# Interleaved rotary embedding, one core: six batch rows on chip instead of five, VectorE in pieces of four positions

## Chip, cores, metric

One core of a Trainium2 chip. The metric is the device time of one execution in microseconds, the median of several; lower is better.

## The reference

`x` is (8, 2048, 16, 64) in float32: 8 batch rows, 2048 positions, 16 heads, 64 values a head. `cos` and `sin` are (2048, 32). Each neighbouring pair of a head is rotated by its position's angle:

```python
x1, x2 = x_pairs[..., 0], x_pairs[..., 1]
out1 = x1 * cos - x2 * sin
out2 = x1 * sin + x2 * cos
out = np.stack([out1, out2], axis=-1).reshape(batch, seq_len, num_heads, head_dim)
```

Input and output are 67.1 MB each, one batch row 8.39 MB each way.

## The kernel before

Partition p holds positions 16p to 16p + 15 (K = 16) of a batch row, 16,384 values. A row comes in through a DMA that GpSimd issues (line 57) and that turns float32 into bf16 on the way; it is rotated in place by VectorE and goes out through a DMA that GpSimd issues (line 60), which turns bf16 into float32. `buf` holds NX = 5 rows of 32 KB a partition, and `at` says in which place a batch row lies; rows 5, 6 and 7 reuse the places of rows 0, 1 and 2.

`rotate` does a stretch of positions in three VectorE operations: the product with the sine table into `qt` (line 79), the product with the cosine table in place (line 85), and the sum of the latter and the pairwise swapped `qt` in place (line 91). Both tables are built in bf16 from cos and sin at the start (lines 104 to 106), with the sign of the sine in the table.

Two pieces of row 0 and row 7 go separately. The first four positions of row 0 come in as float32 through a DMA of ScalarE's queue, beside GpSimd's, and VectorE casts them (line 102). The last four positions of row 7 are summed straight into float32 (`tail`) and go out through SyncE's queue (line 136). A copy of one element before them (line 134) makes them wait for the store of row 6.

The order is written out by hand (`manual_schedule`): each engine runs its own instructions in the order of the text, and a DMA waits on its issuing engine for what it depends on. So GpSimd's order is also the order of its DMA queue: loads of 0 (less the four positions), cos, sin, 1, 2; store 0; loads 3 and 4 as one, 5; stores 1 and 2 as one, 3; loads 6 and 7 as one; stores 4 and 5 as one, 6, 7 (less the last four positions).

When the first store is issued is set by a gate: in the first product of row 1, after 14 of 16 positions (GATE), VectorE copies one element of row 0 onto itself (line 84), and the store of row 0 depends on that copy.

Of the kernel before, what the change touches and what calls it, by code (L numbers as in the profile page):

```python
# [2 lines left out]

# [4 lines left out]


@with_exitstack  # L10
def kernel(
    ctx: ExitStack,
    tc: tile.TileContext,
    x: bass.AP,
    cos: bass.AP,
    sin: bass.AP,
    out: bass.AP,
):
    nc = tc.nc
    fp32 = mybir.dt.float32  # L20
    bf16 = mybir.dt.bfloat16
    mult = mybir.AluOpType.mult
    add = mybir.AluOpType.add

    B, S, H, D = x.shape
    P = 128
    K = S // P
    D2 = D // 2
    HD = H * D
    NX = 5  # L30
    HEAD = 4
    TAIL = 4
    GATE = 14

    x_t = x.rearrange("b (p k) h d -> p b k (h d)", p=P, k=K)
    out_t = out.rearrange("b (p k) h d -> p b k (h d)", p=P, k=K)
    cos_t = cos.rearrange("(p k) c -> p (k c)", p=P, k=K)
    sin_t = sin.rearrange("(p k) c -> p (k c)", p=P, k=K)

    consts = ctx.enter_context(tc.tile_pool(name="consts", bufs=1))  # L40
    rows_pool = ctx.enter_context(tc.tile_pool(name="rows", bufs=1))
    stage = ctx.enter_context(tc.tile_pool(name="stage", bufs=1))

    cos_sb = consts.tile([P, K * D2], fp32)
    sin_sb = consts.tile([P, K * D2], fp32)
    c_tab = consts.tile([P, K, D], bf16)
    s_tab = consts.tile([P, K, D], bf16)


    buf = rows_pool.tile([P, NX, K, HD], bf16, name="xt")  # L50
    at = [4, 0, 1, 2, 3, 4, 0, 1]

    def place(b, n=1, k0=0, k1=K):
        return buf[:, at[b] : at[b] + n, k0:k1]

    def load(b, n=1, k0=0, k1=K):
        nc.gpsimd.dma_start(out=place(b, n, k0, k1), in_=x_t[:, b : b + n, k0:k1])  # L57

    def store(b, n=1, k0=0, k1=K):
        nc.gpsimd.dma_start(out=out_t[:, b : b + n, k0:k1], in_=place(b, n, k0, k1))  # L60

    def rotate(b, k0=0, k1=K, gate=None, to=None):
        nk = k1 - k0
        xp = buf[:, at[b], k0:k1]
        qt = stage.tile([P, K, HD], bf16, name="qt", tag="work")

        def rows(a):
            return a.rearrange("p k (h e) -> p k h e", h=H, e=D)

        def tab(a, j0=0, j1=nk):  # L70
            return dataclasses.replace(
                a,
                offset=a.offset + (k0 + j0) * D,
                ap=[a.ap[0], [D, j1 - j0], [0, H], [1, D]],
            )


        for a, z in ((0, nk),) if gate is None else ((0, GATE), (GATE, nk)):
            nc.vector.tensor_tensor(  # L79
                out=rows(qt[:, a:z]), in0=rows(xp[:, a:z]), in1=tab(s_tab, a, z), op=mult  # L80
            )
            if z < nk:
                one = buf[:1, at[gate], 0, :1]
                nc.vector.tensor_copy(out=one, in_=one)  # L84
        nc.vector.tensor_tensor(out=rows(xp), in0=rows(xp), in1=tab(c_tab), op=mult)  # L85
        q_swap = dataclasses.replace(
            qt, offset=qt.offset + 1, ap=[qt.ap[0], [2, nk * HD // 2], [-1, 2]]
        )
        x3 = xp.rearrange("p k (a j) -> p (k a) j", j=2)
        y3 = x3 if to is None else to.rearrange("p k (a j) -> p (k a) j", j=2)  # L90
        nc.vector.tensor_tensor(out=y3, in0=x3, in1=q_swap, op=add)  # L91

    with tc.manual_schedule():
        head = stage.tile([P, TAIL, HD], fp32, name="st", tag="work")
        nc.scalar.dma_start(out=head[:, :HEAD], in_=x_t[:, 0, :HEAD])
        load(0, k0=HEAD)
        nc.gpsimd.dma_start(out=cos_sb, in_=cos_t)  # L97
        nc.gpsimd.dma_start(out=sin_sb, in_=sin_t)  # L98
        load(1)
        load(2)  # L100

        nc.vector.tensor_copy(out=buf[:, at[0], :HEAD], in_=head[:, :HEAD])  # L102
        s2 = s_tab.rearrange("p k (i j) -> p (k i) j", j=2)
        nc.vector.tensor_copy(out=s2[:, :, 0], in_=sin_sb)  # L104
        nc.vector.tensor_scalar_mul(s2[:, :, 1], sin_sb, -1.0)  # L105
        nc.vector.tensor_copy(  # L106
            out=c_tab.rearrange("p k (i j) -> p (k i) j", j=2),
            in_=cos_sb.to_broadcast([P, K * D2, 2]),
        )

        rotate(0, 0, HEAD)
        rotate(0, HEAD, K)
        rotate(1, gate=0)
        store(0)
        load(3, 2)
        load(5)
        rotate(2)
        store(1, 2)
        rotate(3)
        store(3)  # L120
        load(6, 2)
        rotate(4)
        rotate(5)
        store(4, 2)
        rotate(6)
        store(6)
        rotate(7, 0, K - TAIL)
        store(7, k1=K - TAIL)

        tail = buf[:, at[3], : 2 * TAIL].rearrange("p k e -> p (k e)").bitcast(fp32)
        tail = tail.rearrange("p (k e) -> p k e", e=HD)
        nc.vector.tensor_copy(out=buf[:1, at[6], 0, :1], in_=buf[:1, at[7], K - 1, :1])  # L134
        rotate(7, K - TAIL, K, to=tail)
        nc.sync.dma_start(out=out_t[:, 7, K - TAIL :], in_=tail)


# [1 line left out]
_INS = ['x', 'cos', 'sin']  # L140
_OUTS = [((8, 2048, 16, 64), 'float32')]


# [23 lines left out]
```

## Time and profile before

| | |
|---|---|
| median of 3 runs | 316.18 us (316.11 to 316.2) |
| profiled execution, its own time | 316.17 us |
| its span, first to last instruction | 314.4 us |
| VectorE (DVE) busy | 215.4 us, 37 instructions |
| GpSimd (POOL) busy | 8.6 us, 18 instructions |
| DMA, GpSimd's queue (q0) | 2400 packets, 96.8% of the 16 engines' span |
| DMA, ScalarE's and SyncE's queues (q10, q1) | 144 packets each, 1.8% and 1.6% |
| HBM | 67.63 MB read, 67.11 MB written |

The profile's page has 40 equal slices of the span with the busy share of each engine in tenths. The timeline names each instruction with its start, its duration and, in brackets, the idle time of its engine before it and what ended that. A line number is that of the kernel it belongs to; the change moves lines, so the same operation has another number afterwards.

### The profile page before, as it was taken

The page shows a single profiled execution, that of the slowest core. Times are in us where ns is not written, and L with a number is a line of the kernel's source. Part 1 is how long each engine was busy: PE and PEld are TensorE (multiplying, and loading weights), DVE is VectorE, ACT ScalarE, POOL GpSimd, SP SyncE. Part 2 cuts the span into 40 slices and gives each one's busy share as a digit, 9 for nine tenths or more (in the row PEclk, how much of TensorE's full clock was granted, in tenths as well). Part 3 has the DMA queues.
Part 4 walks back from the last instruction along what each step waited for, and adds up shares of the span by engine and source line. Part 5 has one row for each costly group of instructions (what it writes and reads, how often), then busy time and mean ns, then how long its engine had stood idle before and what let it go on. Part 6 is the DMA issues. An engine that isn't in the chain of part 4 may idle for free.

```text
span 314.4 us, 113 instructions
## 1 busy us (share of the span) xinstructions
DVE 215.4 (69%) x37; POOL 8.6 (3%) x18
## 2 busy tenths in 40 slices
DVE  0029999999999206999999999300009999980550
POOL 3000000100000000000000000000000000000000
DMA  8999999999999999999999999999999999999996
GB/s 253 264 284 200 200 204 263 267 400 417 317 200 200 208 258 200 200 284 517 400 400 475 459 400 400 242 225 200 200 300 434 400 400 534 400 400 400 434 500 267
DMA packets 2688, 102.24 MB, mean 325 GB/s; under 512 B 256, under 2 KB 256, under 8 KB 384
## 3 DMA queue, kind: packets, MB, share of 16 engines
q0 software_dynamic: 2400, 98.04, 96.8%
q10 hardware_dynamic: 144, 2.10, 1.8%
q1 hardware_dynamic: 144, 2.10, 1.6%
HBM read 67.63 MB, written 67.11 MB: 429 GB/s over the span
## 4 chain that ended last, share of the span: by engine, by line
DVE 62%; another core or an unknown queue 17%; DMA 17%; issue 0%; POOL 0%; DVEq 0%; PEldq 0%
DVE xt L91 21%; DVE xt L85 20%; DVE qt L79 20%; DMA out_dram<-xt 10%; DMA sin_sb<-in_sin_dram 7%; POOL xt L57 0%; DVE c_tab L106 0%; POOL cos_sb L97 0%; DVE s_tab L104 0%; DVE s_tab L105 0%; DVE xt L134 0%; DVE xt L84 0%; DVEq L79 0%; PEldq L162 0%
## 5 line engine op out<-in xcount | busy, mean ns | idle before, releaser
L79 DVE TENSOR_TENSOR qt<-xt,s_tab 128x16384 bf16<-128x16384 bf16 (+4 forms) x11 | 69.9, 6360 | 53.7 <-DMA xt<-in_x_dram 53.5
L91 DVE TENSOR_TENSOR xt<-xt,qt 128x16384 bf16<-128x16384 bf16 (+3 forms) x10 | 72.0, 7198 | 0.3
L85 DVE TENSOR_TENSOR xt<-xt,c_tab 128x16384 bf16<-128x16384 bf16 (+2 forms) x10 | 69.9, 6986 | 0.3
L102 DVE CAST xt<-st 128x4096 bf16<-128x4096 f32 x1 | 2.3, 2295 | 15.2 <-DMA st<-in_x_dram 15.2
L60 POOL DMA_DIRECT2D out_dram<-xt x6 | 3.6, 604 | 221.0 <-DVE xt L91 165.3
L134 DVE COPY xt<-xt 1x1 bf16<-1x1 bf16 x1 | 0.1, 144 | 12.0 <-DMA out_dram<-xt 12.0
L57 POOL DMA_DIRECT2D xt<-in_x_dram x6 | 3.8, 635 | 53.1 <-DMA out_dram<-xt 52.3
L104 DVE CAST s_tab<-sin_sb 128x512 bf16<-128x512 f32 x1 | 0.5, 451 | 6.3 <-DMA sin_sb<-in_sin_dram 6.3
L106 DVE CAST c_tab<-cos_sb 128x1024 bf16<-128x1024 f32 x1 | 0.7, 682 | 0.0
L98 POOL DMA_DIRECT2D sin_sb<-in_sin_dram x1 | 0.6, 562 | 0.0
L97 POOL DMA_DIRECT2D cos_sb<-in_cos_dram x1 | 0.6, 554 | 0.0
L105 DVE TENSOR_SCALAR s_tab<-sin_sb 128x512 bf16<-128x512 f32 x1 | 0.4, 441 | 0.0
L84 DVE COPY xt<-xt 1x1 bf16<-1x1 bf16 x1 | 0.1, 136 | 0.0
L151 POOL MEMSET const-float32-0.0<- 128x1 f32 x1 | 0.1, 98 | 0.2 <-issue 0.2
L151 POOL MEMSET const-bfloat16-1.0<- 128x1 bf16 x1 | 0.1, 101 | 0.0
L151 POOL MEMSET const-float32-1.0<- 128x1 f32 x1 | 0.1, 98 | 0.0
L151 POOL MEMSET const-uint8-127<- 128x1 uint8 x1 | 0.1, 98 | 0.0
## 6 DMA issues: line engine op xcount, KB each, us to landing
xt<-in_x_dram POOLq DMA_DIRECT2D x2, 8192.0 KB, 58.7
xt<-in_x_dram POOLq DMA_DIRECT2D x3, 4096.0 KB, 57.4
out_dram<-xt POOLq DMA_DIRECT2D x1, 6144.0 KB, 26.2
xt<-in_x_dram POOLq DMA_DIRECT2D x1, 3072.0 KB, 21.2
st<-in_x_dram ACTq DMA_DIRECT2D x1, 2048.0 KB, 14.5
out_dram<-xt SPq DMA_DIRECT2D x1, 2048.0 KB, 10.2
cos_sb<-in_cos_dram POOLq DMA_DIRECT2D x1, 256.0 KB, 21.3
sin_sb<-in_sin_dram POOLq DMA_DIRECT2D x1, 256.0 KB, 21.4
```

The source lines that it names most:

```text
L57: nc.gpsimd.dma_start(out=place(b, n, k0, k1), in_=x_t[:, b : b + n, k0:k1])
L60: nc.gpsimd.dma_start(out=out_t[:, b : b + n, k0:k1], in_=place(b, n, k0, k1))
L79: nc.vector.tensor_tensor(out=rows(qt[:, a:z]), in0=rows(xp[:, a:z]), in1=tab(s_tab, a, z), op=mult)
L85: nc.vector.tensor_tensor(out=rows(xp), in0=rows(xp), in1=tab(c_tab), op=mult)
L91: nc.vector.tensor_tensor(out=y3, in0=x3, in1=q_swap, op=add)
L97: nc.gpsimd.dma_start(out=cos_sb, in_=cos_t)
L98: nc.gpsimd.dma_start(out=sin_sb, in_=sin_t)
L102: nc.vector.tensor_copy(out=buf[:, at[0], :HEAD], in_=head[:, :HEAD])
L104: nc.vector.tensor_copy(out=s2[:, :, 0], in_=sin_sb)
L105: nc.vector.tensor_scalar_mul(s2[:, :, 1], sin_sb, -1.0)
L106: nc.vector.tensor_copy(out=c_tab.rearrange("p k (i j) -> p (k i) j", j=2), in_=cos_sb.to_broadcast([P, K * D2, 2]),)
L151: nc = _bacc.Bacc("TRN2", target_bir_lowering=False, num_devices=1)
```

## The change

`buf` has six places. Rows 0 to 5 have a place each, and rows 6 and 7 reuse those of rows 0 and 1. GpSimd's order becomes: loads of 0, cos, sin, 1, 2 and 3 as one, 4 and 5 as one; stores 0 and 1 as one, 2 and 3 as one; loads 6 and 7 as one; stores 4 and 5 as one, 6, 7. To find the room, `qt` holds four positions (KP) instead of sixteen, so that every row is rotated in four pieces, three VectorE operations each; and the float32 head, cos and sin lie in row 5's place until the tables are made, so that the load of rows 4 and 5 stands behind the tables. The gate moves to the second piece of row 3, after one position, and holds back the store of rows 0 and 1.

```diff
-    NX = 5
+    NX = 6
+    KP = 4
-    GATE = 14
+    GATE = 1
...
-    cos_sb = consts.tile([P, K * D2], fp32)
-    sin_sb = consts.tile([P, K * D2], fp32)
...
-    at = [4, 0, 1, 2, 3, 4, 0, 1]
+    at = [0, 1, 2, 3, 4, 5, 0, 1]
...
-        qt = stage.tile([P, K, HD], bf16, name="qt", tag="work")
+        qt = stage.tile([P, KP, HD], bf16, name="qt", tag="work")
...
-        head = stage.tile([P, TAIL, HD], fp32, name="st", tag="work")
-        nc.scalar.dma_start(out=head[:, :HEAD], in_=x_t[:, 0, :HEAD])
+
+        def fp32_in(b, k0, k1):
+            return buf[:, at[b], k0:k1].rearrange("p k e -> p (k e)").bitcast(fp32)
+
+        head = fp32_in(5, 0, 2 * HEAD).rearrange("p (k e) -> p k e", e=HD)
+        cos_sb = fp32_in(5, K - 2, K - 1)
+        sin_sb = fp32_in(5, K - 1, K)
+        nc.scalar.dma_start(out=head, in_=x_t[:, 0, :HEAD])
...
         load(1)
-        load(2)
+        load(2, 2)
...
-        rotate(0, 0, HEAD)
-        rotate(0, HEAD, K)
-        rotate(1, gate=0)
-        store(0)
-        load(3, 2)
-        load(5)
-        rotate(2)
-        store(1, 2)
-        rotate(3)
-        store(3)
+        load(4, 2)
+
+        def rotate_row(b, k1=K, gate=None):
+            for k in range(0, k1, KP):
+                rotate(b, k, k + KP, gate if k == KP else None)
+
+        rotate_row(0)
+        rotate_row(1)
+        rotate_row(2)
+        rotate_row(3, gate=0)
+        store(0, 2)
+        store(2, 2)
         load(6, 2)
-        rotate(4)
-        rotate(5)
+        rotate_row(4)
+        rotate_row(5)
         store(4, 2)
-        rotate(6)
+        rotate_row(6)
         store(6)
-        rotate(7, 0, K - TAIL)
+        rotate_row(7, K - TAIL)
         store(7, k1=K - TAIL)
...
-        tail = buf[:, at[3], : 2 * TAIL].rearrange("p k e -> p (k e)").bitcast(fp32)
-        tail = tail.rearrange("p (k e) -> p k e", e=HD)
+        tail = fp32_in(3, 0, 2 * TAIL).rearrange("p (k e) -> p k e", e=HD)
```

More of the change, by code (lines that the diff above doesn't have):

```diff
@@ L99 @@
         load(1)
-        load(2)
-        nc.vector.tensor_copy(out=buf[:, at[0], :HEAD], in_=head[:, :HEAD])
+        load(2, 2)
+        nc.vector.tensor_copy(out=buf[:, at[0], :HEAD], in_=head)
         s2 = s_tab.rearrange("p k (i j) -> p (k i) j", j=2)
```

## The prediction, made before the changed kernel ran

> **What bounds the kernel now.** I read the page's slices and queues first. In the slices, each digit is the busy share of the 16 DMA engines in a fortieth of the span.
>
> ```profile
> DMA  8999999999999999999999999999999999999996
> ...
> q0 software_dynamic: 2400, 98.04, 96.8%
> ...
> HBM read 67.63 MB, written 67.11 MB: 429 GB/s over the span
> ```
>
> The DMA engines are busy from the first slice to the last, nearly all on one queue, the one GpSimd fills. VectorE is busy 69%, so it can only matter where it makes a queue run empty. The second view is a table of stretches: start and end, length, VectorE busy, GpSimd busy, clock, DMA share, GB/s.
>
> ```profile
> 81.20:139.10 57.90, 41.68 (x6) 1.27 (x2) 1.00 1.00 216
> 139.10:197.10 58.00, 57.80 (x7) 1.27 (x2) 1.00 1.03 437
> ```
>
> The first stretch is loads alone (rows 3, 4, 5), the second stores alone (rows 1, 2, 3). Three rows take 58 us either way. The load's GB/s is half because it is counted in the 2-byte values that land; a row is 8.39 MB in memory in both directions. Third, the timeline (start, duration, instruction, in brackets the idle time before it), to see whether the queue ever ran dry.
>
> ```profile
> 25.13 2.28 DVE L79 TENSOR_TENSOR qt<-xt,s_tab 128x4096 bf16<-128x4096 bf16 x1
> 27.45 2.29 DVE L85 TENSOR_TENSOR xt<-xt,c_tab 128x4096 bf16<-128x4096 bf16 x1
> 29.77 2.29 DVE L91 TENSOR_TENSOR xt<-xt,qt 128x4096 bf16<-128x4096 bf16 x1
> 32.10 6.56 DVE L79 TENSOR_TENSOR qt<-xt,s_tab 128x12288 bf16<-128x12288 bf16 x1
> ...
> 51.88 7.63 DVE L79 TENSOR_TENSOR qt<-xt,s_tab 128x14336 bf16<-128x14336 bf16 x1
> 59.42 0.14 DVE L84 COPY xt<-xt 1x1 bf16<-1x1 bf16 x1
> 59.48 1.20 DVE L79 TENSOR_TENSOR qt<-xt,s_tab 128x2048 bf16<-128x2048 bf16 x1
> 59.85 0.54 POOL L60 DMA_DIRECT2D out_dram<-xt  x1 [55.77 <-DVE xt L84]
> 60.38 0.72 POOL L57 DMA_DIRECT2D xt<-in_x_dram  x1
> 60.72 8.69 DVE L85 TENSOR_TENSOR xt<-xt,c_tab 128x16384 bf16<-128x16384 bf16 x1
> ...
> 82.22 0.56 POOL L57 DMA_DIRECT2D xt<-in_x_dram  x1 [21.11 <-DMA out_dram<-xt]
> ...
> 120.40 8.69 DVE L79 TENSOR_TENSOR qt<-xt,s_tab 128x16384 bf16<-128x16384 bf16 x1 [16.08 <-DMA xt<-in_x_dram]
> ...
> 178.60 0.71 POOL L57 DMA_DIRECT2D xt<-in_x_dram  x1 [31.20 <-DMA out_dram<-xt]
> ...
> 236.27 8.69 DVE L79 TENSOR_TENSOR qt<-xt,s_tab 128x16384 bf16<-128x16384 bf16 x1 [37.37 <-DMA xt<-in_x_dram]
> ...
> 294.20 0.14 DVE L134 COPY xt<-xt 1x1 bf16<-1x1 bf16 x1 [12.01 <-DMA out_dram<-xt]
> ```
>
> Five of these start when a transfer lands, so they are marks on the DMA's own clock. From 82.22 (row 0 stored) to 178.60 (rows 1, 2 stored) five rows pass: 96.38 us, 19.28 a row. From 120.40 to 236.27 six rows pass: 115.87, 19.31 a row. From 178.60 to 294.20 six again: 115.60, 19.27. One rate, whether the stretch is mostly loads or mostly stores and wherever VectorE stands: the queue never waited. The packet records agree: the first packet starts at 1.75 us, the last ends at 313.1, and between them an engine is idle for 0.3 us on average. Sixteen row transfers of 19.31 us are 308.9; with 1.75 before and 1.3 after the last packet, 2.4 of the span's 314.4 are left, for the tables (0.52 MB, 1.2 us at that rate) and the head's first packets, which are slow. The profiled execution took 316.17, its span and 1.77 around it; the median is 316.18, so the sum may be read against either.
>
> **The change part by part.** It moves the same bytes. Only a gap in the queue can cost, and only the head, the end or the rate could give. So I follow the queue.
>
> Start: head, cos and sin land at other addresses, with the same sizes and the same issuing engines. 0 us. Loads of rows 4 and 5 overwrite the place of head and tables, so that issue now waits for VectorE's last table copy, at about 25.2 us. Behind it on GpSimd stands only the first store, due at 117 us. The queue then holds rows 1 to 3, 3 x 19.3 us, until 81.3. The cover is 56 us. 0 us. Nearly five rows are then queued at once, where before about four were the most (at 199.2 us: nearly two rows to load, two to store). Should GpSimd have to hold that issue back until a row has drained, the same 56 us cover it.
>
> VectorE's pieces: an operation on four positions starts 2.32 us after the one before it (25.13, 27.45, 29.77, 32.10), so a piece takes 6.97 and a row 27.88, against 3 x 8.73 = 26.2 for a whole row (8.69 each and the step to the next, 0.03). That is 1.7 us more a row, 12 us at most in all, off the path unless a store is late.
>
> The first store, the one tight place. Rows 0 and 1: 25.13 + 8 x 6.97 = 80.89. Rows 2 and 3 now come as one transfer. Counting back from 120.40 over three rows (0 out, 3 and 4 in), VectorE could have started on row 2 at 62.5; one row later is 81.78, so VectorE waits 0.9 us. Row 2 ends at 81.78 + 27.88 = 109.66, row 3's first piece at 116.63. The gate then lies behind one position of the next multiply (1,024 elements, about 0.67 us by the 1.20 of 2,048; the copy starts just before its end): 117.2. GpSimd took the issue 0.43 us after the copy's start (59.42 to 59.85): 117.64. The packet records have the first packet of that store at 61.72 us, 1.87 after the issue, on a DMA engine that had been empty for 0.15 us; so 1.87 is a real latency. One row's issue took 0.54 us and two rows' 0.71; if that 0.17 adds, it is 2.04. The first packet of the new store is due at 119.5 to 119.7. The engines finish their loads between 61.57 and 62.02 in the old trace; three rows, 57.9 us, later is 119.5 to 119.95. The engines that end last set the end, and for them the store is 0.25 to 0.45 us early. Cost 0, with a first packet that may be up to 0.2 late on the earliest engines. I take 1.87 to 2.04, because it is the same kind of issue in the same place. The bounds of this latency are 0 below and 4.1 above: the first load was issued at 1.24 and its first packet is at 5.31, behind packets of the other queue. At 4.1 the store comes at 121.7, 1.8 us after the last engine is empty.
>
> The rest of the queue: stores 0, 1 run 119.9 to 158.5. Row 3 is ready at 117.2 + 1.8 for the rest of the multiply + 2 x 2.32 + 2 x 6.97 = 137.6: stores 2, 3 are queued 21 us early and run to 197.1. Loads 6, 7 wait for stores 0, 1, are issued near 159 and are 38 us early; what stands behind them on GpSimd is the store of rows 4, 5, which VectorE has ready only at 137.6 + 55.8 = 193.4, against a need at 235.7. Rows 6, 7 land at 236.2 as before. Row 6 is ready at 264.2, needed at 274.3; row 7's twelve positions at 264.2 + 20.9 = 285.1, needed at 293.6. The covers there are 10 and 8 us. The last four positions wait for row 6's store, 294.2 as before, and are the same three instructions. End: unchanged.
>
> Direction changes of the queue, on GpSimd's order, fall from five to three, and its DMAs from fourteen to twelve. The nearest row: the stretch to 236.27 has one row and one DMA more than the stretch to 178.60 and is 19.49 us longer, 0.2 above a row at most. The packet records put a border between two DMAs at 0.02. I take 2 x 0.02 = 0.04 us, bounded by 0 and 0.4. [...]
>
> The sum: 316.17 + 0 - 0.04, so 316.2. A measurement of this kernel can tell about 0.2%, 0.63 us, from no change.
>
> **The rivals.** *The gate comes late (slower).* Place: the store of rows 0, 1 behind row 3's second piece. Price: one us for every us that its first packet comes after 119.95. It decides over the 0.63 us from a latency of about 2.9 us; at the first load's 4.1 the time is 318.0. For: nothing else is left in the queue there, and a two-row store is the first store of its shape. Against: 1.87 measured, with VectorE equally busy. If descriptors had to wait for the running multiply, the old store's first packet was 1.04 after its end (60.68 to 61.72), and the new one, whose multiply of three positions ends near 119.0, would come at 120.0: 316.2 still, with the margin gone. [...] Chance 0.12, reaching to 318.0.
>
> *Larger, fewer DMAs give time back (faster).* [...] Against: three stretches at one rate. Chance 0.03.
>
> *VectorE becomes the bound.* The smallest later cover is 8 us at row 7, over 49 us of pieces: they would have to be 17% slower than 2.32 us. Past that, each us is a us. Chance 0.01, slower.
>
> **How the numbers follow.** Forecast, no change: 0.84, at 316.2, its own range 315.9 to 316.8. Gate late or VectorE late: 0.13, of it about half under 317.0. Faster: 0.03. The range 315.9 to 317.0 takes the forecast case and the nearer half of the late gate. Faster 0.03, same 0.84, slower 0.13.
>
> **What would show it.** Right: the new trace's first store issue near 117.6, row 2's first multiply near 81.8, VectorE's waits on loads in two places (0.9 us before row 2, and some 43 us before row 6, from 193.4 to 236.2, apart from the head), last copy at 294.2, span 314.4, VectorE busy near 226. Wrong: a stretch behind the gate in which the DMA digit falls below 9, row 6's first multiply later than 236.9, or a stretch whose row takes other than 19.3 us.

## The result, and the profile after

The changed kernel takes 316.67 us (median of 22 runs, 316.45 to 317.22) against 316.18 (22 runs, 316.0 to 316.32). The ratio is 1.0017, 95% interval 1.0011 to 1.0024: half a microsecond slower, less than the 0.63 us of the prediction's bound but clear of zero. The forecast of no change within 0.2% held; the sum behind it, 0 less 0.04, did not.

The page of the changed kernel, the lines that answer to those of before, and one more:

```profile
span 314.9 us, 176 instructions
...
DVE 225.9 (72%) x103; POOL 7.9 (2%) x16
...
DMA  7999999999999999999999999999999999999996
...
q0 software_dynamic: 2368, 98.04, 96.6%
...
q14 instruction: 2, 0.01, 0.0%
HBM read 67.63 MB, written 67.11 MB: 428 GB/s over the span
```

The span is 0.5 us longer, the DMA engines are still busy in every slice, the bytes are the same. The line `q14 instruction` is new: two packets, nearly all of it one of 8 KB, on a queue that the profile of before does not list. There, HBM follows on q1:

```profile
q1 hardware_dynamic: 144, 2.10, 1.6%
HBM read 67.63 MB, written 67.11 MB: 429 GB/s over the span
```

Beside VectorE's count of instructions (103, before 37) it is the only line of the page that hints at the cause.

The table of stretches (start and end, length, VectorE busy, GpSimd busy, clock, DMA share, GB/s): loads of rows 4 and 5, then stores of rows 0 to 3, of the changed kernel.

```profile
81.30:119.80 38.50, 37.45 (x19) 0.70 (x1) 1.00 0.97 211
119.80:197.30 77.50, 72.71 (x32) 2.13 (x3) 1.00 1.04 437
```

The rates are nearly those of before (216 and 437): two rows of loads in 38.5 us are 19.25 us a row, four rows of stores in 77.5 are 19.4. The timeline of the changed kernel (start, duration, instruction, idle time before it), at the places that the prediction named:

```profile
81.81 2.29 DVE L78 TENSOR_TENSOR qt<-xt,s_tab 128x4096 bf16<-128x4096 bf16 x1 [0.86 <-DMA xt<-in_x_dram]
...
117.31 0.14 DVE L83 COPY xt<-xt 1x1 bf16<-1x1 bf16 x1
...
117.75 0.70 POOL L59 DMA_DIRECT2D out_dram<-xt  x1 [91.50 <-DVE xt L83]
...
138.02 0.72 POOL L59 DMA_DIRECT2D out_dram<-xt  x1 [19.56 <-DVE xt L90]
...
160.02 0.70 POOL L56 DMA_DIRECT2D xt<-in_x_dram  x1 [21.29 <-DMA out_dram<-xt]
...
236.87 2.29 DVE L78 TENSOR_TENSOR qt<-xt,s_tab 128x4096 bf16<-128x4096 bf16 x1 [43.30 <-DMA xt<-in_x_dram]
...
294.79 0.14 DVE L140 COPY xt<-xt 1x1 bf16<-1x1 bf16 x1 [9.10 <-DMA out_dram<-xt]
```

Until the first store the clock of the transfers is nearly that of before (81.81, forecast 81.78). Rows 6 and 7 land 0.60 us later (236.87 against 236.27), and that lateness stays to the end (294.79 against 294.20). The packet records of the trace place it. The 8 KB packet of q14 runs at 144.05 us for 0.34 us. On one of the 16 DMA engines a store packet had started at 141.64, and as such packets start 2.41 us apart, the next was due at 144.05; it starts at 144.39 and takes 2.785 us, where all others take 2.449: that engine loses about 0.34 and again 0.34, 0.67 us in all. The engine that was last by then had started its packet at 141.82, so 0.67 - 0.18 = 0.49 us of it is lateness against all others. It is the last engine from then on: it ends its loads of rows 6 and 7 at 236.48, the others by 235.98, and row 6's first multiply starts 0.39 us after it, as it started 0.43 us after the last engine before (235.84); its last 48 KB packet ends at 308.90, those of the others by 308.40.

### The profile page after: what moved, and what is told of

It reads as the page before. It is cut to its first block, busy times and chain, and to the rows that moved or that the text cites. A ratio compares the mean times of both kernels' runs of the same rounds, so it can differ in the third digit from the quotient of the medians.

```text
span 314.9 us, 176 instructions
## 1 busy us (share of the span) xinstructions
DVE 225.9 (72%) x103; POOL 7.9 (2%) x16
## 4 chain that ended last, share of the span: by engine, by line
DVE 65%; DMA 16%; another core or an unknown queue 14%; issue 1%; POOL 0%; DVEq 0%; PEldq 0%
DVE xt L90 22%; DVE xt L84 21%; DVE qt L78 21%; DMA out_dram<-xt 9%; DMA xt<-in_sin_dram 7%; POOL xt L56 0%; DVE c_tab L111 0%; POOL xt L102 0%; DVE s_tab L109 0%; DVE s_tab L110 0%; DVE xt L140 0%; DVE xt L83 0%; DVEq L78 0%; PEldq L168 0%
## 5 line engine op out<-in xcount | busy, mean ns | idle before, releaser
L78 DVE TENSOR_TENSOR qt<-xt,s_tab 128x4096 bf16<-128x4096 bf16 (+2 forms) x33 | 73.4, 2226 | 45.1 <-DMA xt<-in_x_dram 44.2
L90 DVE TENSOR_TENSOR xt<-xt,qt 128x4096 bf16<-128x4096 bf16 (+1 forms) x32 | 75.5, 2359 | 1.1
L84 DVE TENSOR_TENSOR xt<-xt,c_tab 128x4096 bf16<-128x4096 bf16 x32 | 73.4, 2292 | 1.1
L107 DVE CAST xt<-xt 128x4096 bf16<-128x4096 f32 x1 | 2.3, 2294 | 15.3 <-DMA xt<-in_x_dram 15.3
L111 DVE CAST c_tab<-xt 128x1024 bf16<-128x1024 f32 x1 | 0.7, 684 | 0.0
```

Of the source, the lines that this page charges most:

```text
L78: nc.vector.tensor_tensor(out=rows(qt[:, a:z]), in0=rows(xp[:, a:z]), in1=tab(s_tab, a, z), op=mult)
L107: nc.vector.tensor_copy(out=buf[:, at[0], :HEAD], in_=head)
L111: nc.vector.tensor_copy(out=c_tab.rearrange("p k (i j) -> p (k i) j", j=2), in_=cos_sb.to_broadcast([P, K * D2, 2]),)
```

## The experiments

**Theory A:** 66 more VectorE instructions (103 against 37 on the pages; the expectations count the waits and barriers of the program too, 121 against 52) make the chip fetch one more block of the program during the run, through a DMA engine that has no free time (the page's DMA digits are 9 but at the ends). That the 8 KB packet is such a block is read from the name of its queue, `instruction`; the runs test whether it goes with the number of instructions. **Rivals:** B, the first store; C, the order, the larger DMAs or the small pieces themselves.

*e1, 70 more instructions, nothing else.* The kernel before, with one-element copies in VectorE's idle time:

```diff
+    idle = consts.tile([P, 70], bf16)
...
         rotate(5)
         store(4, 2)
+        for i in range(70):
+            nc.vector.tensor_copy(out=idle[:1, i : i + 1], in_=c_tab[:1, 0, :1])
```

> The kernel before with 70 one-element copies on VectorE, put between row 5 and row 6, where VectorE was idle for 37 us; nothing waits for them. VectorE's program is then as long as that of the changed kernel (122 instructions against 121, 52 before). Theory A (the longer VectorE program makes the chip fetch one more block of instructions during the run, an 8 KB packet on queue q14, which the profile of the changed kernel shows and that of before does not, and which holds up one of the 16 DMA engines): a q14 packet inside the span and the time up by 0.3 to 0.6 us, to 316.5 to 316.8. Theory B (the late first store of the changed kernel costs it) and theory C (its row order, larger DMAs or pieces of four do): 316.2, no change.

316.51 us, ratio 1.0010 (1.0001 to 1.0019), 0.37 us above the kernel before on the same chip. The page has `q14 instruction: 1, 0.01, 0.0%`. That is the packet and the time of A; B and C had no change and no packet.

*e2, 330 copies.*

> The same with 330 copies in the same place (some 21 us by the 0.06 us step after the old gate's copy, inside the 37 us of idle time), so 382 instructions. Theory A: two or three fetches of 8 KB inside the span; if all fall on one DMA engine, the time is up by two to three times what 70 copies cost, 316.9 to 317.8; if on different engines, it is up only by about as much as with 70. Theories B and C: 316.2, as long as the copies end before row 6 lands.

317.52 us, ratio 1.0049 (1.0036 to 1.0063), 1.38 us above its kernel before (316.14). Its page, and under it two lines of its timeline:

```profile
span 315.6 us, 443 instructions
...
q14 instruction: 3, 0.02, 0.0%
```

```profile
198.74 20.01 DVE L127 COPY idle<-c_tab 1x1 bf16<-1x1 bf16 x330
...
237.53 8.69 DVE L80 TENSOR_TENSOR qt<-xt,s_tab 128x16384 bf16<-128x16384 bf16 x1 [18.78 <-DMA xt<-in_x_dram]
```

VectorE waited 18.78 us for row 6 behind the copies, so they delayed nothing themselves; three packets cost 0.46 us each, and row 6 landed 1.26 us later than before. They stand at 204.15, 211.92 and 219.69 us, 7.77 apart, which is 128 copies of 20.01 / 330 = 0.0606 us. The spacing is also that of three load packets (2.41 us each) and the 0.53 us that a fetch adds: here, as in the changed kernel, e1, e8 and e10, the fetch starts where its DMA engine's next packet was due. So two spacings, 15.54 us, are known only to within one packet; if each packet is the next block of VectorE's program, a block of 8 KB is 128 instructions to within about 20, an estimate from these three packets. All three met the same DMA engine: one ends the loads of rows 6 and 7 at 237.13 us, the other fifteen between 235.50 and 235.75.

*e3, the changed kernel with 15 instructions fewer*, rows 6 and 7 in whole rows, the sine product going to row 2's place:

```diff
...
-        rotate_row(6)
+        free = buf[:, at[2]]
+        rotate(6, qt=free)
...
-        rotate_row(7, K - TAIL)
+        rotate(7, 0, K - TAIL, qt=free[:, : K - TAIL])
```

> The changed kernel with rows 6 and 7 rotated in whole rows again, the sine product going to the place of row 2, which is stored by then; 15 VectorE instructions fewer (106). Order of loads and stores, the gate and rows 0 to 5 stay as they are. Theory A: the program is back under one block, no q14 packet of 8 KB inside the span, 316.2. Theories B and C: 316.7, as the changed kernel.

316.72 us, ratio 1.0023 (1.0014 to 1.0032), no gain. It still had its q14 packet, at 142.1 us, so it did not tell A from C; my idea that 106 instructions would need no fetch was wrong. e10 and e12 asked when the fetch comes.

*e4, the changed kernel without its gate:* `rotate_row(3, gate=3)`, the copy on an element of row 3 itself.

> The changed kernel with the gate's copy made on an element of row 3 itself, so that it holds nothing back: the store of rows 0 and 1 is issued when row 1 is done, near 81 us instead of 117.7, and waits in the queue. Same number of instructions. Theory B: back to 316.2. Theories A and C: 316.7, with the q14 packet still there.

317.63 us, ratio 1.0046 (1.0033 to 1.0059): neither side. An earlier first store makes it slower by 0.96 us, where I had taken an early issue as free. So this run doesn't decide on B. The trace of the changed kernel does: its first store packet follows the last load packet on its engine without a gap (at 119.74), so the store was not late and B falls as the cause of the half microsecond. A new question stands, why an early store costs.

*e8, pieces of four in the order of before*, with the gate's copy put where the first store's issue stays at 59.73 us (59.85 before):

```diff
...
+        def rotate_row(b, k1=K, gate=None):
+            for k in range(0, k1, KP):
+                rotate(b, k, k + KP, gate if k == 0 else None)
...
```

> The kernel before, five places and its own order of loads and stores, with VectorE in pieces of four positions; the gate's copy is put where the issue of the first store falls within 0.1 us of where it was (in the sum of row 1's first piece, behind three of four positions). Theory A (the fetch that the longer VectorE program brings is the cost): a q14 packet of 8 KB in the span and 316.5 to 316.7. Theory C (the order with six rows and two-row DMAs is the cost): 316.2.

316.51 us, ratio 1.0012 (1.0003 to 1.0021), with one packet of 8 KB at 124.7 us: as e1. Five places and the old order cost the same as six and the new one, within the intervals, once the instructions are as many. C falls, to the 0.1 us that these runs can't tell apart. In the profiled execution the engine that fetched ends its loads of rows 6 and 7 at 236.32, 0.29 us after the others; slightly longer load packets, of which more below, may make up the rest.

*e10 and e12, 20 and 8 copies:* when is the block fetched, and do copies alone cost?

> The kernel before with 20 one-element copies between rows 5 and 6, 72 VectorE instructions instead of 52 (with 122 and with 106 a fetch was seen). Theory H (the next block is fetched when about half of the 128 instructions of the first are used up, whether it is needed or not): an 8 KB q14 packet near 204 us and 316.5. Theory I (it is fetched only near the end of the block): none, 316.15.

> The kernel before with 8 copies between rows 5 and 6 instead of 20 or 70: 60 VectorE instructions. With 20 the fetch's packet came at 242.8 us, when VectorE was 2 or 3 instructions behind the wait for row 6, so some 50 instructions into its program without its barriers; with 8 copies that place is never reached. Theory A with H (the fetch is the cost, and it comes when about half a block is used up): no q14 packet in the span and 316.15, as before. If the copies themselves cost something: 316.2 to 316.4 without a packet.

With 20 copies: 316.67 us, ratio 1.0018 (1.0008 to 1.0027), and a packet, not near 204 but at 242.8 us, after row 6 had landed. By the estimate of 128, 72 instructions are little over half a block, and the packet came all the same; where a block begins in VectorE's program no run shows. The copies cost nothing themselves: the stretch that they stand in is as long as without them to 0.03 us (57.70 in the table below), and the loss comes in the stretch of the packet. With 8: no packet, 316.31 us, ratio 1.0005 (0.9996 to 1.0014). That is not to be told from no change; its median is 0.2 above the kernel before and its median span 0.1 (314.4 against 314.3), and whether either is real stays open. Nor do these runs fix the point of the fetch as a count of instructions: by the records in the traces, waits and barriers among them, VectorE had started 50 of 116 when the packet ran in e8, 56 of 70 in e10 and 63 of 115 in the changed kernel, and e12 ran all of its 58 without one. The pages of e10 and of e12:

```profile
span 314.8 us, 133 instructions
...
q14 instruction: 1, 0.01, 0.0%
```

```profile
span 314.3 us, 121 instructions
...
q1 hardware_dynamic: 144, 2.10, 1.6%
HBM read 67.63 MB, written 67.11 MB: 429 GB/s over the span
```

In e12 no line stands between q1 and HBM. The spans sort by packets: 314.4 (before) and 314.3 (e12) with none, 314.8 (e8, e10), 314.9 (the changed kernel) and 315.0 (e1) with one, 315.6 (e2) with three.

The marks on the transfers' clock put the cost where the packet is. Each number is the difference of two starts in the timeline: loads 6, 7 issued (GpSimd), row 6's first multiply, last copy. The kernel before has 57.67 and 57.93.

| run | q14 packets at | issue to row 6 | row 6 to last copy |
|---|---|---|---|
| before | none | 57.67 | 57.93 |
| e12, 8 copies | none | 57.70 | 57.89 |
| e1, 70 copies | 204.6 | 58.08 | 57.89 |
| e2, 330 copies | 204.2, 211.9, 219.7 | 59.04 | 57.90 |
| e10, 20 copies | 242.8 | 57.70 | 58.41 |

A stretch without a packet is as long as before to 0.04 us; one packet adds 0.41 or 0.48, three add 1.37. For e10 the last two marks are these, in its timeline:

```profile
236.26 8.69 DVE L80 TENSOR_TENSOR qt<-xt,s_tab 128x16384 bf16<-128x16384 bf16 x1 [36.17 <-DMA xt<-in_x_dram]
...
294.67 0.14 DVE L137 COPY xt<-xt 1x1 bf16<-1x1 bf16 x1 [12.48 <-DMA out_dram<-xt]
```

**The gate.** *e6, the gate 3.8 us later*, behind the cosine product:

```diff
         nc.vector.tensor_tensor(out=rows(xp), in0=rows(xp), in1=tab(c_tab), op=mult)
+        if gate is not None:
+            one = buf[:1, at[gate], 0, :1]
+            nc.vector.tensor_copy(out=one, in_=one)
...
```

> The changed kernel with the gate's copy moved behind the cosine product of the same piece, 4.0 us later (116.7 + 2 x 2.33 = 121.4 against 117.3). By the prediction's price (one us for every us that the first packet comes after the last engine is empty, latency 1.87 to 2.04 from the issue): issue near 121.8, first packet at 123.6 to 123.9, all engines empty from 120.1 at the latest, so 3.5 to 3.8 us above the changed kernel's 316.7: 320.2 to 320.5. If instead the latency is that of the run's first load (4.1): 322.5.

319.64 us, ratio 1.0113 (1.0097 to 1.0128): 2.97 above the changed kernel, where 3.5 to 3.8 was expected. GpSimd's line in its timeline:

```profile
121.53 0.70 POOL L59 DMA_DIRECT2D out_dram<-xt  x1 [95.41 <-DVE xt L84]
```

The packet records have the first packet at 122.79, the last engine's first at 122.95: the latency of this two-row store into an empty queue is 1.26 to 1.42 us, not 1.87 to 2.04. The last engine had ended its loads at 119.91 and stood for 3.05 us, and the kernel lost 2.97: the price of one us a us is right.

*e5, the kernel before without its gate* (`rotate(1, gate=1)`), *e7 and e11, the changed kernel's gate 7 and 3 us earlier* (in row 3's first piece, e7 behind one position, e11 behind the cosine product).

> The kernel before with its gate's copy made on an element of row 1 instead of row 0, so that it holds nothing back: the store of row 0 and the loads of rows 3 and 4 behind it are issued when row 0 is done, near 52 us, 10 us before the queue runs dry, instead of 59.85. Theory D (a first store that is already queued while the last loads ahead of it run costs about 1 us where the queue turns from loads to stores, as the changed kernel without its gate showed: 317.63 against 316.67): 317.1, with the last load packet of each DMA engine about 1 us long. Theory E (in a queue that runs in order an early issue costs nothing, and what that run showed comes from something of the changed kernel's, its five queued rows or its two-row store): 316.2.

> The changed kernel with the gate in the first piece of row 3 instead of the second: the store of rows 0 and 1 is issued near 110.8 us, 9 us (about four packets of each DMA engine) before the queue runs dry. Theory D: 317.6, as without the gate. Theory E: 316.7.

> The changed kernel with the gate's copy behind the cosine product of row 3's first piece: the store of rows 0 and 1 is issued near 114.7 us, 3 us earlier than in the changed kernel and 4 later than in the run that took 317.49. With the latency of 1.26 us that the late gate showed, its first packet is ready at 116.0, when each DMA engine still has its last load packet ahead of it (those begin at 117.2 to 117.7). If the store must not be queued before the last load packet begins: 317.5. If only a longer lead costs: 316.7.

All three lose as without a gate: e5 317.40 (ratio 1.0041, 1.0027 to 1.0054), e7 317.49 (1.0044, 1.0031 to 1.0056), e11 317.60 (1.0046, 1.0031 to 1.0061). Theory D holds in its times; the last load packets are about 1 us longer, not 1 us long. GpSimd's lines of e5, to be read against 59.85 and 82.22 in the kernel before:

```profile
52.08 0.54 POOL L60 DMA_DIRECT2D out_dram<-xt  x1 [47.99 <-DVE xt L91]
52.61 0.72 POOL L57 DMA_DIRECT2D xt<-in_x_dram  x1
83.33 0.56 POOL L57 DMA_DIRECT2D xt<-in_x_dram  x1 [30.00 <-DMA out_dram<-xt]
```

The store is issued 7.8 us earlier and done 1.1 later. In the packet records the last load packet of each DMA engine takes 3.2 to 4.1 us in e5 and 3.1 to 3.7 in e4, e7 and e11, where it takes 2.43 in the kernel before and 2.43 to 2.49 in the changed one. Issued at 114.61 (e11) the loss is whole, at 117.75 (the changed kernel) it is not there: the last load packets begin at 117.2 to 117.7. Later changes from loads to stores, at 139 and 235 us, show no such packets in the kernel before (the last load packets take 2.43 us there too), although their stores are issued over 30 us ahead (104.62 and 199.20).

*e9, is it the first write to memory of the run?* e5 with a tiny store through SyncE's queue early:

```diff
         load(2)
+        nc.sync.dma_start(out=out_t[:, 7, K - 1, :16], in_=cos_sb[:, :16])
...
```

> The kernel before without its gate, as in the run that took 317.40, and with one tiny store added early: SyncE writes 128 x 64 bytes of the cos table to the last position of row 7, which the last store overwrites at the end. It waits for the cos table, so it runs near 24 us, among the loads. Theory F (what costs 1.3 us is the first write to memory of the run, paid once by each DMA engine): 316.2 to 316.5, with the last load packets before the first big store back at 2.43 us, or the same loss moved to 24 us (then 317.4 and slow packets there). Theory G (it is the state of GpSimd's own queue, or the place written to): 317.4, with the slow packets where they were.

317.34 us, ratio 1.0040 (1.0025 to 1.0055); the tiny packets run from 27.9 us on, and the slow load packets stay where they were (3.1 to 3.8 us). The early write by SyncE's queue did not pay for it (317.34 against 317.40 in e5): F falls. Whether it is the first store of GpSimd's own queue, or the place it writes to, is open.

## Why the prediction was right, and where its sum was not

The forecast, no change within 0.2%, came true, but not by its reasons alone: the sum missed a cost of 0.49 us, which happened to be less than the 0.63 us that it could tell from no change. Of its own signs of being wrong, row 6's first multiply at 236.87 us stayed 0.03 us short of the 236.9 named; the span was 0.5 us longer and the last copy 0.6 us later than it said.

*What bounds the kernel:* right. The DMA engines stay full; every experiment that moved the time did it by taking time from one or all of them, and at the rates forecast (the stretches of loads and of stores run nearly as before, 19.25 and 19.4 us a row).

*The changes at the start and VectorE's pieces:* right. The load of rows 4, 5 was issued at 25.52 us (forecast 25.2); VectorE's busy time is 225.9 us (226), its waits for loads before rows 2 and 6 are 0.86 and 43.30 us (0.9 and 43). e8 shows that the pieces cost nothing beyond their number.

*The gate:* right in place and cost, off in one term. The copy came at 117.31 (117.2) and the issue at 117.75 (117.64); the first store packet follows the last load packet on its engine without a gap, at 119.74. The latency, 1.87 to 2.04 in the sum, is 1.26 to 1.42 by e6. Nor did the store wait there for the running VectorE operation, the case that the prediction weighed: its first packet came at 122.79, inside a sum that ran from 121.20 to 123.49. I had read the 0.15 us for which one DMA engine stood empty in the kernel before as proof of the latency; if an issue needs 1.3 us, that store was ready at about 61.1 us, before any engine ran empty, and the 0.15 has another cause, which was not tried. So the margin on the late side was about 1 us (issue at 117.75, ready at 119.01 to 119.17, the last engine's loads done at 120.13), not 0.25 to 0.45, and the rival of the late gate was less near than its chance said.

*What the prediction left out at the gate:* it priced lateness alone. Early has a price too, 0.8 to 1.3 us (e4, e5, e7, e11), and the changed kernel's issue at 117.75 lies in a window that begins after 114.6 (e11) and, by the latency of e6, ends about 1 us behind 117.75. It cost nothing here, which as far as the sum goes was luck: GpSimd's queue runs in order, and e5's store, issued 7.8 us earlier, still cost 1.26 us.

*The rest of the queue:* right. The covers were 20 us (138.02 against 158), 37, 42, 9 and 8 us; none was used up.

*Borders and directions, 0.04 us:* not to be seen in these runs. Two DMAs and two changes of direction fewer gave nothing back that shows: the median is 0.49 us up, and the fetch accounts for that to within 0.1 us.

*The step that failed* is the claim that only a gap in the queue can cost. The 66 added instructions were counted as VectorE's time alone. By the estimate from e2 (8 KB for about 128) they are also some 4 KB more program, and the changed kernel, e1, e2, e3, e8 and e10 each show packets of 8 KB on q14 within the run, the kernel before and e12 none. A fetch took 0.53 to 0.54 us from its DMA engine among loads (e1, e2, e8) and 0.67 among stores (the changed kernel, e10), and the kernel loses that less what the engine was ahead of the last one: 0.37 us in e1 and e8, 0.46 a packet in e2, 0.54 in e10, against 0.49 for the change. That accounts for it within the intervals. What may be left, about 0.1 us, goes with slightly longer load packets before the first store in the profiled execution (1.3 us in all, 0.08 an engine; e8 has 2.2 in all); such packets come and go between executions (the kernel before has none, e3's profile ten times as much), and their cause was not tried.

VectorE showed no loss from a fetch: the 330 copies of e2, with two of the three packets inside, took 20.01 us, 0.0606 each; the 70 of e1, done before its packet, took 4.30, 0.0614 each. The loss is that of the DMA engine, which in this kernel has no idle time to bring the packet in (0.3 us on average between the first packet and the last of the kernel before).

No version beat the kernel before: it has no fetch within its span, and its first store is issued at 59.85 us, just after the last load packet of each DMA engine began (59.14 to 59.59).

## What to carry to other kernels

When the DMA engines are the bound, count the instructions that a change adds, also on an engine that has time (VectorE here): each 8 KB packet of q14 took 0.53 to 0.67 us from one DMA engine here, and as row 6's multiply started 0.39 to 0.43 us after the last engine's load, with or without a fetch, the kernel lost 0.37 to 0.54 a packet. Splitting work into more, smaller instructions was not free: the kernel before in pieces of four (e8) took 316.51 us against 316.14, with VectorE still waiting 32.45 us for row 6. Look for the q14 line of the page first when a DMA-bound kernel moves by a fraction of a us without a gap. And test the issue time of a run's first store on both sides: too late cost about a us for every us here (e6: 2.97 us for 3.05), too early 0.8 to 1.3 us (e4, e5, e7, e11).

## What was not expected of the hardware

- Packets of 8 KB on q14, the queue that the page names `instruction`, ran among the loads and stores and cost the kernel 0.37 to 0.54 us each. Their number went with VectorE's program: none with 60 instructions (e12), one with 72 (e10) and with 122 (e1), three with 382 (e2). The three of e2 are 7.77 us apart at 0.0606 us a copy, by which a packet is some 128 instructions, an estimate.
- With the first store of GpSimd's queue issued before the last load packets began, the last load packet of each DMA engine took 3.1 to 4.1 us (e4, e5, e7, e11); issued just after they began, it took 2.43 us (the kernel before, 59.85 against 59.14 to 59.59) and 2.43 to 2.49 (the changed kernel, 117.75 against 117.27 to 117.68). At the later changes to stores of the kernel before, at 139 and 235 us, it took 2.43.
- The latency of a two-row store from GpSimd's issue to the first packet was 1.26 us on the first DMA engine and 1.42 on the last, with an empty queue and VectorE busy (e6).
